# Last feed-forward of a two-layer streaming encoder: two of seven sums per group added by VectorE, and state products over all 128 rows

## The chip, the cores and the metric

The kernel runs on one core of a Trainium2 chip. The metric is device time in microseconds of one execution; lower is better. One further execution was recorded by the hardware profiler, and all rows below come from that one.

The engines are named as in the profile: PE is TensorE (PEld its weight loads), DVE is VectorE, ACT is ScalarE, POOL is GpSimd, and SP is SyncE, which here only issues DMAs.

## What is computed

Two layers of an encoder are applied to 640 token rows (512 of a new stream, 8 x 16 of running streams) of width 1024. Each layer is a feed-forward, a mixer and another feed-forward, and every sub-layer is wrapped in a layer norm. The change lies in the last feed-forward, and in the sample states of the second layer's mixer, which are computed beside it:

```python
def swiglu(x, w_gate, w_up, w_down):
    return (jax.nn.silu(x @ w_gate) * (x @ w_up)) @ w_down
...
x = layer_norm(ALPHA * x + 0.5 * swiglu(x, ffn_w_gate[l, 1], ffn_w_up[l, 1], ffn_w_down[l, 1]),
               ln_g[l, 2], ln_b[l, 2])
...
h_new = h * jnp.exp(cs[:, -1])[..., None, None] + jnp.einsum('bsgr,bsgn,bsgrp->bgrpn', to_end, b_c, x_c)
```

The inner width of the feed-forward, 2816, is 22 tiles of 128. In `h_new`, each of 4 head groups and 8 running streams has a state of 128 x 512 and 16 new tokens.

## The kernel before

All matrices are fp32. Each is split into a high and a low part, and a product is three matmuls: high x high, low x high, high x low. ACT casts the high part (line 94) and DVE subtracts for the low part (line 95). The activations stay in SBUF: `xt` with channels on partitions, and `yacc`, the running sum with tokens on partitions, five token tiles of 128 by 1024.

A feed-forward (`ffn`) goes over the 22 inner tiles: the first two by themselves, then five groups of four. Gate and up projections are made for two tiles at a time with Strassen's scheme in seven products instead of eight (`matrix`, line 356). The down projection of a group of four is made while the next group's weights arrive. In three of the four feed-forwards (`SEVEN`), the groups but the last use seven products too: `down7`. The last feed-forward, `ffn3`, has four such groups.

`down7` first makes token tile 4 in the plain way (line 506, summed on line 509). The other four token tiles are two pairs: `tp` 0 holds tiles 0 and 1, `tp` 1 holds tiles 2 and 3. The seven products `p` come in the order 1, 2, 5, 6, 3, 7, 4, each for `tp` 0 and then `tp` 1, six matmuls of 128x512 each (line 488). They share three accumulators per pair: `x` (products 1, 6, 7, 4), `w` (5, 3) and `z` (2). `x` and `w` come from the four PSUM banks of kind `b`, `z` from those of kind `a`. After each product, `add` puts the accumulator as it stands onto one half `j` of one token tile of `yacc`; only then may the next product of the chain go on accumulating in it. The tiles and halves for the products in their order are, for `tp` 0: (0, 0), (0, 0), (1, 1), (0, 1), (0, 1), (1, 1), (1, 0).

`add` has two ways:

- for `tp` 1 (`t // 2` is 1): one DVE instruction reads PSUM, scales and adds to `yacc` (line 496);
- for `tp` 0: ACT copies the scaled accumulator to a buffer `ev` (line 499), and POOL sends a DMA that adds it to `yacc` (line 500). Where side work runs (`few`, in the first and the last feed-forward) there are two `ev` buffers, elsewhere three. A DMA that adds to a tile's half waits for an earlier one on the same half to land.

Beside `ffn3` runs `ssd_states`, a generator that is moved on one step at a `tick` (in `down7` after product 5 and after product 3, and before it). It goes over 4 head groups x 2 x 2, 16 steps; a step loads rows for two streams, `h` 0 and 1, into `xb`: at rows 64h, three blocks of 16 rows (high x high, high x low, low x high: x parts in columns 0 to 511, b parts in 512 to 639). For each of the two streams it then makes one fp32r product over 48 rows, rows 64h to 64h + 47 of `xb` (line 1149), into a bank of kind `b`; ACT scales the old state `h0` in eight pieces (line 1152), DVE adds (line 1153), and SP stores it (line 1154).

The order of instructions on each engine is fixed when the kernel is built, by a scheduler that goes by estimated durations; each engine then runs its list in order.

Of the kernel before, what the change touches and what calls it, by code (L numbers as in the profile page):

```python
# [9 lines left out]
F32 = mybir.dt.float32  # L10
F32R = mybir.dt.float32r
# [24 lines left out]
def kernel(ctx: ExitStack, tc: tile.TileContext, I, O, phases=PHASES):  # L36
    nc = tc.nc

    def pool(name, bufs=1, stack=ctx, **kw):
        return stack.enter_context(tc.tile_pool(name=name, bufs=bufs, **kw))  # L40
# [24 lines left out]
    def bank_a():  # L65
        return bank("a")

    def bank_b():
        return bank("b")
# [27 lines left out]
    def raw_tile():  # L97
        return pools["raw"].tile([128, 1024], F32, name="raw")
# [4 lines left out]
    def two_units():  # L103
        return pools["w"].tile([128, 2, 2, 512], F32R, name="w")

    def split2(w, src):

        return split(w[:, :, 0], w[:, :, 1], src.rearrange("p (j c) -> p j c", j=2))
# [19 lines left out]
    def mm3(ps, lhs, rhs):  # L128
        n = 3 * len(lhs)
        k = 0  # L130
        for (wh, wl), (xh, xl) in zip(lhs, rhs):
            for a, b in ((wh, xh), (wl, xh), (wh, xl)):
                state["pe"] = nc.tensor.matmul(ps, a, b, start=(k == 0), stop=(k == n - 1)).ins  # L133
                k += 1
# [76 lines left out]
    def ffn(i, ph, last, side=None):  # L211
# [4 lines left out]
        with ExitStack() as st:  # L216
            wk = pool(f"ffn{i}_wk", 1, st, reuse_waits="tile")
            few = side is not None
            steps = side(wk) if side is not None else iter(())

            def tick(where):

                if ph == "ffn0" and where in range(NT):
                    for _ in range(2 if (fs[0], where) == (14, 4) else 1):
                        with tc.issue_after(state["acc"]):
                            next(steps, None)
                elif ph == "ffn3" and where in ("gate", "up", 0, 2, 4):
                    with tc.issue_after(state["silu"]):
                        next(steps, None)
# [48 lines left out]
            for r in range(2):  # L278
                w = load_w(I["w_gate"][i, 2 + r])
                first[r] = g_row()  # L280
                for c in range(2):
                    p = bank_a()[:, :Q]
# [166 lines left out]
            def down7(fs):  # L449


                raws, direct = {}, {}
                for f in fs:
                    raws[f] = raw_tile()
                    nc.sync.dma_start(raws[f], I["w_down"][i, f])
                for f in fs:
                    direct[f] = two_units()
                    split2(direct[f], raws[f])

                for f in fs[::2]:  # L460
                    (b11, b12), (b21, b22) = ((r[:, :512], r[:, 512:]) for r in (raws[f], raws[f + 1]))
                    V.tensor_tensor(b22, b22, b12, op=ALU.subtract)
                    V.tensor_tensor(b12, b12, b11, op=ALU.subtract)
                    V.tensor_tensor(b11, b22, b11, op=ALU.add)
                    V.tensor_tensor(b21, b21, b11, op=ALU.subtract)
                T = {}
                for r in range(2):
                    for f in fs[::2]:
                        T[f + r] = two_units()
                        split2(T[f + r], raws[f + r])  # L470

                def left(f, p, tp):
                    tok = lambda k, a: ht[f + k][:, :, 256 * tp + 128 * a:256 * tp + 128 * a + 128]
                    if p in (1, 2, 4):
                        return tok(*{1: (0, 0), 2: (1, 0), 4: (1, 1)}[p])
                    o = 256 * {5: 0, 6: 1, 7: 2, 3: 3}[p] + 128 * tp
                    return hs[f][:, :, o:o + 128]

                def right(f, p):
                    return {1: direct[f][:, 0], 2: direct[f + 1][:, 0], 3: direct[f + 1][:, 1],  # L480
                            6: T[f][:, 0], 5: T[f][:, 1], 4: T[f + 1][:, 0], 7: T[f + 1][:, 1]}[p]

                def product(ps, tp, p, first):
                    n = 0
                    for f in fs[::2]:
                        a, b = left(f, p, tp), right(f, p)
                        for u, v in ((0, 0), (1, 0), (0, 1)):
                            nc.tensor.matmul(ps, a[:, u], b[:, v], start=(first and n == 0), stop=(n == 5),  # L488
                                             skip_group_check=True)
                            n += 1  # L490

                def add(ps, t, j):

                    if t // 2:
                        ya = yacc[:, t, j * 512:j * 512 + 512]
                        V.scalar_tensor_tensor(ya, ps, 0.5 / ALPHA, ya, op0=ALU.mult, op1=ALU.add)  # L496
                        return
                    e = wk.tile([128, 512], F32, name="ev", bufs=2 if few else 3)
                    nc.scalar.mul(e, ps, 0.5 / ALPHA)  # L499
                    nc.gpsimd.dma_start(yacc[:, t, 512 * j:512 * j + 512], e, accum_op=ALU.add)  # L500

                t = NT - 1
                tick(0)
                for j in range(2):
                    pb = bank_a()
                    mm3(pb, [(ht[f][:, 0, t * 128:t * 128 + 128], ht[f][:, 1, t * 128:t * 128 + 128]) for f in fs],
                        [(direct[f][:, j, 0], direct[f][:, j, 1]) for f in fs])
                    ya = yacc[:, t, j * 512:j * 512 + 512]
                    state["acc"] = V.scalar_tensor_tensor(ya, pb, 0.5 / ALPHA, ya, op0=ALU.mult, op1=ALU.add).ins
                x, w = ([bank_b() for _ in range(2)] for _ in range(2))  # L510
                z = [bank_a() for _ in range(2)]
                for p, ps, a, j in ((1, x, 0, 0), (2, z, 0, 0), (5, w, 1, 1), (6, x, 0, 1), (3, w, 0, 1), (7, x, 1, 1),
                                    (4, x, 1, 0)):
                    for tp in range(2):
                        product(ps[tp], tp, p, p in (1, 2, 5))
                        add(ps[tp], 2 * tp + a, j)
                    if p in (5, 3):
                        tick(2 if p == 5 else 4)

# [605 lines left out]
    def ssd_states(wk):  # L1125

        el8 = wk.tile([128, 4, 8, 8], F32, name="el8")
        nc.sync.dma_start(el8.rearrange("p g b h -> p g (b h)"), ssd["el"])
        for g, b2, q in ((g, b2, q) for g in range(4) for b2 in range(2) for q in range(2)):

            xb = wk.tile([128, 640], F32, name="xb", bufs=1)
            for h in range(2):
                for r, (sx, sb) in enumerate(((0, 0), (0, 1), (1, 0))):
                    rows = slice(64 * h + 16 * r, 64 * h + 16 * r + 16)
                    t0 = 64 * h + 32 * b2 + 16 * q
                    src = lambda s, a, b: ssd["xb"][g][s, t0:t0 + 16, a:b]
                    if sx == sb:
                        nc.sync.dma_start(xb[rows], src(sx, 0, 640))
                    else:
                        nc.sync.dma_start(xb[rows, 0:512], src(sx, 0, 512))  # L1140
                        nc.sync.dma_start(xb[rows, 512:640], src(sb, 512, 640))
            for h in range(2):
                n = 4 * h + 2 * b2 + q
                h0 = wk.tile([128, 512], F32, name="h0", bufs=1)
                nc.sync.dma_start(h0, I["ssd_h0"][g, n])
                yield
                rows = slice(64 * h, 64 * h + 48)
                pst = bank_b()
                nc.tensor.matmul(pst, xb[rows, 512:640].bitcast(F32R), xb[rows, 0:512].bitcast(F32R),  # L1149
                                 start=True, stop=True)  # L1150
                for k in range(8):
                    nc.scalar.mul(h0[:, 64 * k:64 * k + 64], h0[:, 64 * k:64 * k + 64], el8[:, g, n, k:k + 1])  # L1152
                nc.vector.tensor_tensor(h0, h0, pst, op=ALU.add)
                nc.sync.dma_start(O["ssd_s"][g, n], h0)
# [391 lines left out]
    for ph in phases:  # L1546
        last = ph == phases[-1]
        if ph.startswith("ffn"):
            ffn(int(ph[3]), ph, last, sides.get(ph))
        elif ph == "mix0":  # L1550
            mixer0(ph, last)
        else:
            mixer1(ph, last)
            if "ffn3" not in phases:
                with ExitStack() as st:
                    for _ in ssd_states(pool("ssd", 1, st, reuse_waits="tile")):
                        pass
# [112 lines left out]
```

## Time and profile before

| | |
|---|---|
| Time, median of 3 runs | 2623.69 us (2619.67 to 2629.86) |
| Profiled execution, time | 2620.05 us |
| Profiled execution, span of the trace | 2618.4 us |
| Last feed-forward in the trace | from about 2150 us to the end |
| Its four `down7` groups | near 2262 to 2292, 2346 to 2376, 2430 to 2460, 2517 to 2547 us |
| State products, line 1149 | 32, from 2191.9 to 2557.1 us |
| ACT copies of line 499, whole kernel | 84, median 0.597 us |
| Adding DMAs of line 500, whole kernel | 84, from issue to landing 3.2 / 4.2 / 8.0 us (least, median, most) |

A row of the timeline gives the start in us from the start of the span, the duration, the engine, the line of the kernel, the operation and "output <- input"; in square brackets, how long the engine stood idle before it and what ended that. A matmul's row gives the rows and columns of its weights (128\*128) and then the moving operand. Matmuls overlap, so the distance from start to start counts for them, not the duration. The granted clock is TensorE's, 1.00 at full speed.

### The profile page before, as it was taken

The page shows a single profiled execution, that of the slowest core. Times are in us where ns is not written, and L with a number is a line of the kernel's source. Part 1 is how long each engine was busy: PE and PEld are TensorE (multiplying, and loading weights), DVE is VectorE, ACT ScalarE, POOL GpSimd, SP SyncE. Part 2 cuts the span into 40 slices and gives each one's busy share as a digit, 9 for nine tenths or more (in the row PEclk, how much of TensorE's full clock was granted, in tenths as well). Part 3 has the DMA queues.
Part 4 walks back from the last instruction along what each step waited for, and adds up shares of the span by engine and source line. Part 5 has one row for each costly group of instructions (what it writes and reads, how often), then busy time and mean ns, then how long its engine had stood idle before and what let it go on. Part 6 is the DMA issues. An engine that isn't in the chain of part 4 may idle for free. (4 is left out here: it accounts for less than half of the span.)

```text
span 2618.4 us, 41048 instructions
## 1 busy us (share of the span) xinstructions
PE 2532.5 (97%) x15529; PEld 2291.1 (88%) x15529; DVE 2071.7 (79%) x3770; ACT 1312.2 (50%) x2632; POOL 310.0 (12%) x440
## 2 busy tenths in 40 slices
PE   9999999999969999999999999999999999999998
PEld 8999999887658999998999999889999879898887
DVE  7788877667858888887888887777686898787778
ACT  4444344345523555553455554566564544666562
POOL 0000003010021000003000002211111240000001
PEclk9999999999979999999999999999999999999999
DMA  5332334542211334443144433456464722545552
GB/s 180 105 105 91 104 110 138 183 146 75 81 61 49 97 93 125 111 127 108 50 109 124 110 103 121 126 182 220 123 205 140 241 67 89 155 149 149 152 161 97
DMA packets 177846, 324.80 MB, mean 124 GB/s; under 512 B 20416, under 2 KB 91200, under 8 KB 177136
## 3 DMA queue, kind: packets, MB, share of 16 engines
q1 hardware_dynamic: 163792, 293.83, 35.0%
q0 software_dynamic: 13856, 28.35, 5.6%
q8 instruction: 122, 2.00, 0.3%
q14 instruction: 76, 0.62, 0.1%
HBM read 259.56 MB, written 40.54 MB: 115 GB/s over the span
## 5 line engine op out<-in xcount | busy, mean ns | idle before, releaser
L95 DVE TENSOR_TENSOR w<-raw,w 128x512 fp32r<-128x512 f32 (+1 forms) x617 | 553.5, 920 | 95.0 <-ACT w L94 94.1
L94 ACT CAST w<-raw 128x512 fp32r<-128x512 f32 (+1 forms) x617 | 466.0, 794 | 221.1 <-DVE raw L335 75.4
L133 PE MATMUL bank<-xhi,w 128*128 128x256 f32 (+2 forms) x2528 | 555.9, 312 | 14.3 <-ACT xhi L94 7.2
L356 PE MATMUL bank<-xhi,w 128*128 128x320 f32 x2432 | 544.1, 310 | 2.5 <-ACT mx L367 2.2
L133 PEld LDWEIGHTS bank<-xhi,w 128*128 128x128 f32 x2528 | 421.8, 189 | 26.2 <-ACT xhi L94 8.1
L356 PE MATMUL bank<-T,w 128*128 128x320 f32 x2736 | 427.0, 309 | 0.7 <-DVE s L393 0.5
L356 PEld LDWEIGHTS bank<-xhi,w 128*128 128x128 f32 x2432 | 406.4, 188 | 11.9 <-ACT mx L367 5.1
L356 PEld LDWEIGHTS bank<-T,w 128*128 128x128 f32 x2736 | 406.3, 188 | 3.3 <-ACT mx L367 1.2
L133 PE MATMUL bank<-xlo,w 128*128 128x256 f32 (+2 forms) x1264 | 391.3, 310 | 3.7 <-DVE xlo L95 3.6
L356 PE MATMUL bank<-xlo,w 128*128 128x320 f32 x1216 | 375.0, 308 | 0.0
L133 PE MATMUL bank<-w,h 128*128 128x512 f32 x1488 | 348.6, 391 | 0.0
L133 PEld LDWEIGHTS bank<-w,h 128*128 128x128 f32 x1488 | 276.5, 188 | 58.8 <-issue 1.2
L133 PEld LDWEIGHTS bank<-xlo,w 128*128 128x128 f32 x1264 | 238.6, 189 | 6.1 <-DVE xlo L95 4.7
L356 PEld LDWEIGHTS bank<-xlo,w 128*128 128x128 f32 x1216 | 228.1, 188 | 0.4
L500 POOL DMA_DIRECT2D yacc<-ev x84 | 73.0, 897 | 1019.9 <-ACT ev L499 828.6
L367 ACT COPY mx<-bank 128x320 f32<-128x320 f32 x228 | 96.0, 423 | 113.5 <-PE bank L356 111.8
L488 PE MATMUL bank<-w,hs 128*128 128x512 f32 x576 | 142.8, 408 | 0.0
L488 PEld LDWEIGHTS bank<-w,hs 128*128 128x128 f32 x576 | 113.6, 198 | 26.4 <-issue 2.1
L95 DVE TENSOR_TENSOR w<-sw,w 128x1024 fp32r<-128x1024 f32 x76 | 92.9, 1223 | 50.0 <-ACT w L94 49.7
L94 ACT CAST w<-sw 128x1024 fp32r<-128x1024 f32 x76 | 79.8, 1049 | 72.3 <-DVE sw L335 71.2
L496 DVE SCALAR_TENSOR_TENSOR yacc<-bank,yacc 128x512 f32<-128x512 f32 x84 | 57.3, 687 | 67.0 <-PE bank L488 67.0
L208 DVE SCALAR_TENSOR_TENSOR yacc<-bank,yacc 128x512 f32<-128x512 f32 x120 | 81.9, 686 | 35.1 <-PE bank L133 34.6
(416 smaller groups left out, 3531.8 us busy)
## 6 DMA issues: line engine op xcount, KB each, us to landing
raw<-in_w_gate_dram SPq DMA_DIRECT2D x88, 512.0 KB, 4.0
raw<-in_w_up_dram SPq DMA_DIRECT2D x88, 512.0 KB, 4.1
raw<-in_w_down_dram SPq DMA_DIRECT2D x88, 512.0 KB, 3.7
raw<-in_m_in_dram SPq DMA_DIRECT2D x52, 512.0 KB, 4.6
yacc<-ev POOLq DMA_DIRECT2D x84, 256.0 KB, 4.2
raw<-in_m_out_dram SPq DMA_DIRECT2D x24, 512.0 KB, 3.8
csb<-cs_d SPq DMA_DIRECT2D x20, 512.0 KB, 5.3
h<-in_ssd_h_dram SPq DMA_DIRECT2D x16, 512.0 KB, 5.7
```

The costliest lines, as they stand in the source:

```text
L94: nc.scalar.copy(hi, src)
L95: return nc.vector.tensor_tensor(lo, src, hi.bitcast(F32), op=ALU.subtract)
L133: state["pe"] = nc.tensor.matmul(ps, a, b, start=(k == 0), stop=(k == n - 1)).ins
L208: state["acc"] = nc.vector.scalar_tensor_tensor(ya, pb, scale, ya, op0=ALU.mult, op1=ALU.add).ins
L356: nc.tensor.matmul(ps, A[p][:, a, k * 128:k * 128 + 128], B[p][b][:, k, :], start=(first and n == 0), stop=(n == 11), skip_group_check=True)
L367: nc.scalar.copy(e[n], ps)
L488: nc.tensor.matmul(ps, a[:, u], b[:, v], start=(first and n == 0), stop=(n == 5), skip_group_check=True)
L496: V.scalar_tensor_tensor(ya, ps, 0.5 / ALPHA, ya, op0=ALU.mult, op1=ALU.add)
L500: nc.gpsimd.dma_start(yacc[:, t, 512 * j:512 * j + 512], e, accum_op=ALU.add)
```

## The change

Two edits, both only in the last feed-forward.

First, in `add`, products 6 and 7 of the first pair of token tiles take the DVE way too where `few` is set. Of the feed-forwards with side work only `ffn3` uses `down7`, so this is 2 sums in each of 4 groups: 8 copies on ACT and 8 adding DMAs become 8 DVE instructions of line 496.

Second, the state products read all 128 rows. The x parts go to `xrow`, 128 x 512, the b parts to `brow`, one 128 x 128 block for each `h`. Both are set to zero once by DVE. Only rows 64h to 64h + 47 of block `h` of `brow` are ever loaded, so the others stay zero and the product over 128 rows gives the same sum. Each 16-row block is now two loads, so a step has twelve loads where it had ten.

```diff
-                def add(ps, t, j):
+                def add(ps, t, j, p):
-                    if t // 2:
+                    if t // 2 or few and p in (6, 7):
                         ya = yacc[:, t, j * 512:j * 512 + 512]
                         V.scalar_tensor_tensor(ya, ps, 0.5 / ALPHA, ya, op0=ALU.mult, op1=ALU.add)
                         return
...
                         product(ps[tp], tp, p, p in (1, 2, 5))
-                        add(ps[tp], 2 * tp + a, j)
+                        add(ps[tp], 2 * tp + a, j, p)
...
+        xrow = wk.tile([128, 512], F32R, name="xrow", bufs=1)
+        brow = wk.tile([128, 2, 128], F32R, name="brow", bufs=1)
+        nc.vector.memset(xrow.bitcast(F32), 0.0)
+        nc.vector.memset(brow.bitcast(F32), 0.0)
         for g, b2, q in ((g, b2, q) for g in range(4) for b2 in range(2) for q in range(2)):
-            xb = wk.tile([128, 640], F32, name="xb", bufs=1)
             for h in range(2):
                 for r, (sx, sb) in enumerate(((0, 0), (0, 1), (1, 0))):
...
-                    if sx == sb:
-                        nc.sync.dma_start(xb[rows], src(sx, 0, 640))
-                    else:
-                        nc.sync.dma_start(xb[rows, 0:512], src(sx, 0, 512))
-                        nc.sync.dma_start(xb[rows, 512:640], src(sb, 512, 640))
+                    nc.sync.dma_start(xrow[rows].bitcast(F32), src(sx, 0, 512))
+                    nc.sync.dma_start(brow[rows, h].bitcast(F32), src(sb, 512, 640))
...
-                rows = slice(64 * h, 64 * h + 48)
                 pst = bank_b()
-                nc.tensor.matmul(pst, xb[rows, 512:640].bitcast(F32R), xb[rows, 0:512].bitcast(F32R),
-                                 start=True, stop=True)
+                nc.tensor.matmul(pst, brow[:, h], xrow, start=True, stop=True)
```

The scheduler orders the last feed-forward anew. Three places of the first `down7` group show how; groups 1 and 3 are ordered alike, and so are 2 and 4.

ACT, before, from the copy of product 1 (line 499) to the cast of the weight sum `sw` for the next projection; the lines 1152 are the eight scalings of one state, the lines 94 are weight casts:

```order
L499 ACTIVATE ev<-bank 128x512
L1152 ACTIVATE h_22667<-h_22667,el_21897 128x64 x3
L94 CAST w<-raw 128x2x512 x3
L1152 ACTIVATE h_22667<-h_22667,el_21897 128x64 x5
L499 ACTIVATE ev<-bank 128x512 x2
L94 CAST w_22937<-raw 128x512
L94 CAST w<-raw 128x2x512
L499 ACTIVATE ev<-bank 128x512 x2
L94 CAST w<-sw 128x2x512
```

The same stretch of ACT with the change (the scaling is on line 1151 there):

```order
L499 ACTIVATE ev<-bank 128x512
L94 CAST w<-raw 128x2x512 x3
L1151 ACTIVATE h_22675<-h_22675,el_21897 128x64 x8
L499 ACTIVATE ev<-bank 128x512 x2
L94 CAST w_22943<-raw 128x512
L94 CAST w<-raw 128x2x512
L499 ACTIVATE ev<-bank 128x512
L94 CAST w<-sw 128x2x512
```

The copy of product 6 is gone, so that of product 3 stands alone ahead of the cast of `sw`; and all eight scalings stand between the casts and the copies of products 2 and 5, where three of them stood ahead of the casts.

PE, before, from product 5 of the group on; `w,hs` are the matmuls of products 5, 6, 3 and 7, line 1149 the state products, line 356 the next projection:

```order
L488 MATMUL bank<-w,hs 128x512 x34
L1149 MATMUL bank<-xb 128x512
L488 MATMUL bank<-w,hs 128x512 x9
L1149 MATMUL bank<-xb 128x512
L488 MATMUL bank<-w,hs 128x512 x5
L356 MATMUL bank<-xhi,w 128x320 x2
```

The same stretch of PE with the change; `w,h` are the matmuls of product 4:

```order
L488 MATMUL bank<-w,hs 128x512 x34
L1149 MATMUL bank<-xrow,brow 128x512
L488 MATMUL bank<-w,hs 128x512 x8
L1149 MATMUL bank<-xrow,brow 128x512
L488 MATMUL bank<-w,hs 128x512 x6
L488 MATMUL bank<-w,h 128x512 x12
L356 MATMUL bank<-xhi,w 128x320 x2
```

The first state product keeps its place behind 34 of the 48 matmuls. Product 4 now follows product 7 at once; before, nine matmuls of the next projection stood between them.

DVE, before, from the addition of the preceding state to the second sum of product 7 (line 496 is the adding instruction, line 335 the weight sums, line 95 the low parts):

```order
L1153 TENSOR_TENSOR h_22667<-h_22667,bank 128x512
L496 SCALAR_TENSOR_TENSOR yacc<-bank,yacc 128x512 x2
L95 TENSOR_TENSOR w_22937<-raw,w_22937 128x512
L496 SCALAR_TENSOR_TENSOR yacc<-bank,yacc 128x512
L95 TENSOR_TENSOR w<-raw,w 128x2x512
L335 TENSOR_TENSOR sw<-raw 128x512
L335 TENSOR_TENSOR sw<-sw,raw 128x512
L496 SCALAR_TENSOR_TENSOR yacc<-bank,yacc 128x512
L95 TENSOR_TENSOR w<-sw,w 128x2x512
L335 TENSOR_TENSOR raw<-raw,sw 128x512
L496 SCALAR_TENSOR_TENSOR yacc<-bank,yacc 128x512
```

The same stretch of DVE with the change:

```order
L1152 TENSOR_TENSOR h_22675<-h_22675,bank 128x512
L496 SCALAR_TENSOR_TENSOR yacc<-bank,yacc 128x512 x2
L95 TENSOR_TENSOR w_22943<-raw,w_22943 128x512
L496 SCALAR_TENSOR_TENSOR yacc<-bank,yacc 128x512
L95 TENSOR_TENSOR w<-raw,w 128x2x512
L335 TENSOR_TENSOR sw<-raw 128x512
L335 TENSOR_TENSOR sw<-sw,raw 128x512
L496 SCALAR_TENSOR_TENSOR yacc<-bank,yacc 128x512 x2
L95 TENSOR_TENSOR w<-sw,w 128x2x512
L496 SCALAR_TENSOR_TENSOR yacc<-bank,yacc 128x512
```

The two sums behind the state addition are now those of product 5 (`tp` 1) and product 6 (`tp` 0); behind line 335 stand product 3's (`tp` 1) and product 7's (`tp` 0) together, and product 7's second sum follows the low part of `sw`.

## The prediction

> **What bounds the kernel now.** I read the page's first part, then the last feed-forward alone: busy time by windows, who waits for whom on PE, the timeline round one wait. Line 1 gives TensorE's share of the span; the others are stretches of the last feed-forward (length, then busy us of PE, PEld, DVE, ACT, POOL, granted clock, DMA share, GB/s).
>
> ```profile
> PE 2532.5 (97%) x15529; PEld 2291.1 (88%) x15529; DVE 2071.7 (79%) x3770; ACT 1312.2 (50%) x2632; POOL 310.0 (12%) x440
> 2262.00:2292.00 30.00, 25.73 (x110) 20.59 (x109) 21.20 (x29) 15.82 (x33) 6.09 (x7) 0.94 0.70 179
> 2292.00:2346.00 54.00, 54.00 (x344) 50.90 (x343) 46.98 (x73) 36.11 (x83) 0.00 (x0) 1.00 0.44 139
> 2346.00:2376.00 30.00, 27.32 (x111) 21.72 (x110) 20.60 (x27) 16.14 (x34) 6.07 (x7) 0.89 0.79 197
> 2430.00:2460.00 30.00, 25.62 (x103) 19.91 (x103) 20.04 (x28) 15.26 (x32) 5.19 (x6) 0.89 0.66 175
> 2517.00:2547.00 30.00, 26.69 (x109) 21.21 (x108) 20.57 (x27) 16.22 (x34) 6.06 (x7) 0.89 0.78 199
> ```
>
> TensorE is the bound: between the seven-product groups (2292 to 2346) it has no idle time. The four 30-us windows hold one group each, and there it idles 4.27 + 2.68 + 4.38 + 3.31 = 14.64 us, at a mean clock below 1. The longest of PE's waits from 2160 to 2584 (total us, times, longest) says for whom:
>
> ```profile
> PE bank L1149 <- ACT ev L499: 14.6, 4, 4.4
> ```
>
> All of it is one wait per group: the state product of line 1149 needs a `b` bank, and the bank that comes free is the one that ACT reads for product 3. Round the fourth wait (start, us, engine, line, tile; behind it the idle time and its releaser):
>
> ```profile
> 2523.73 7.87 PE L488 MATMUL bank<-w,hs 128*128 128x512 f32 x34
> 2534.91 0.79 PE L1149 MATMUL bank<-xb 48*128 48x512 f32 x1 [3.31 <-ACT ev L499]
> ...
> 2528.08 0.59 ACT L499 ACTIVATE ev<-bank 128x512 f32<-128x512 f32 x1
> 2532.79 0.60 ACT L499 ACTIVATE ev<-bank 128x512 f32<-128x512 f32 x1 [4.12 <-DMA yacc<-ev]
> 2534.26 0.60 ACT L499 ACTIVATE ev<-bank 128x512 f32<-128x512 f32 x1
> ...
> 2520.80 0.87 POOL L500 DMA_DIRECT2D yacc<-ev  x1 [59.16 <-ACT ev L499]
> 2528.29 1.76 POOL L500 DMA_DIRECT2D yacc<-ev  x2 [6.61 <-ACT w L94]
> ```
>
> The three ACT rows are the copies of products 5, 6 and 3 for the first tile pair; the POOL rows send product 1's addition, then those of products 2 and 5. There are two `ev` buffers: product 6 (2532.79) waits until the addition of product 2, sent at 2528.29, has landed, and product 3 (2534.26) stands behind it on ACT. The product of line 1149 starts 0.05 us after that copy ends.
>
> **Part 1: sums 6 and 7 on DVE.** Without product 6 on ACT, product 3 is the fourth user of `ev` and takes the buffer that product 6 took, at its time. So the bank is free when the copy of product 6 ended. The same pairs of copies in groups 1 to 3, with two earlier rows of group 1:
>
> ```profile
> 2266.65 0.83 ACT L1152 ACTIVATE h<-h,el 128x64 f32<-128x64 f32 x3 [1.24 <-DVE raw L464]
> 2271.43 1.05 ACT L499 ACTIVATE ev<-bank 128x512 f32<-128x512 f32 x2
> 2278.55 0.60 ACT L499 ACTIVATE ev<-bank 128x512 f32<-128x512 f32 x1 [3.64 <-DMA yacc<-ev]
> 2280.18 0.60 ACT L499 ACTIVATE ev<-bank 128x512 f32<-128x512 f32 x1 [1.03 <-DMA yacc<-ev]
> ...
> 2361.18 0.60 ACT L499 ACTIVATE ev<-bank 128x512 f32<-128x512 f32 x1 [3.62 <-DMA yacc<-ev]
> 2362.85 0.60 ACT L499 ACTIVATE ev<-bank 128x512 f32<-128x512 f32 x1
> ...
> 2447.88 0.60 ACT L499 ACTIVATE ev<-bank 128x512 f32<-128x512 f32 x1 [3.88 <-DMA yacc<-ev]
> 2449.38 0.60 ACT L499 ACTIVATE ev<-bank 128x512 f32<-128x512 f32 x1 [0.90 <-DMA yacc<-ev]
> ```
>
> Earlier by 1.63, 1.67, 1.50 and 1.47 us. In groups 1 and 3 the order of ACT takes half back: the three scalings that used a gap (2266.65, 0.83 us) now stand with the other five behind the casts, so the copies of products 2 and 5 (2271.43), the addition and its landing come some 0.83 us later. I take 0.8 + 1.67 + 0.67 + 1.47 = **4.6 us** of idle time gone (6.3 without that loss; all 14.6 if the landing also came sooner). The waits left are estimated at 3.5, 1.0, 3.7 and 1.8 us. What is late next is the landing of product 2's addition, which waits for product 1's on the same rows of `yacc`; no part of the change touches that pair.
>
> DVE gets 8 additions (four groups, two sums, one tile of the pair):
>
> ```profile
> L496 DVE SCALAR_TENSOR_TENSOR yacc<-bank,yacc 128x512 f32<-128x512 f32 x28 | 18.8, 686 | 22.6 <-PE bank L488 22.6
> ```
>
> That is 8 x 0.686 = 5.5 us, in windows in which DVE is busy 20 to 21 of 30 us. Product 7's addition waits for product 5's to have landed (same tile and half): group 1 has that at 2280.18, when product 3's copy got product 5's buffer, and product 7 would end about 2281.3, so it passes with about 1 us to spare. Behind it on DVE stand the lower half of the cast sum `sw` and product 7's second sum, for which product 4 waits; between the two lie six matmuls, 1.4 us. I take 0; if that cover goes, 0.7 us a group, 2.7 in all. The two memsets are once, below 1 us.
>
> **Part 2: the clock.** After each wait TensorE runs at half clock (first four rows: the slow stretch in each group). The last three: a short gap elsewhere, a somewhat longer one, and what followed that.
>
> ```profile
> 2281.25:2284.65 3.40, 3.40 (x9) 2.71 (x9) 2.13 (x3) 2.38 (x9) 0.85 (x1) 0.50 0.36 61
> 2363.50:2369.95 6.45, 6.45 (x15) 4.76 (x16) 4.18 (x6) 3.48 (x10) 1.72 (x2) 0.50 0.69 149
> 2450.05:2455.15 5.10, 5.10 (x11) 3.33 (x11) 2.42 (x3) 3.31 (x10) 0.86 (x1) 0.50 0.49 85
> 2534.90:2540.45 5.55, 5.54 (x12) 4.08 (x13) 4.38 (x6) 3.66 (x10) 0.85 (x1) 0.50 0.63 140
> ...
> 1802.00:1804.00 2.00, 0.27 (x3) 0.04 (x2) 1.97 (x7) 1.18 (x4) 0.79 (x4) 1.00 0.60 143
> ...
> 2134.00:2136.50 2.50, 0.43 (x3) 0.32 (x3) 2.50 (x3) 0.00 (x0) 2.42 (x3) 1.00 0.00 0
> 2137.25:2140.65 3.40, 3.22 (x9) 2.52 (x9) 2.87 (x8) 0.00 (x0) 0.48 (x1) 0.59 0.00 0
> ```
>
> 20.5 us at 0.50 cost half of it, 10.25 us. A gap of 1.73 us (2.00 - 0.27) left the clock at 1; one of 2.07 did not. So the edge lies between. Group 2 (1.0 us left) keeps its clock, saving 6.45/2 = 3.2. Group 4 (1.8) lies nearer to 1.73 than to 2.07: 5.55/2 = 2.8 saved. Groups 1 and 3 (3.5, 3.7) stay slow: 0. I take **6.0 us**; ends: 0 and 10.25.
>
> **Part 3: 128 rows.** A 48-row product in an unbroken run, and the pitch of full ones:
>
> ```profile
> 2326.09 1.92 PE L356 MATMUL bank<-T,w 128*128 128x320 f32 x12
> 2327.95 0.50 PE L1149 MATMUL bank<-xb 48*128 48x512 f32 x1
> 2328.38 0.56 PE L356 MATMUL bank<-xhi,w 128*128 128x320 f32 x2
> ...
> 2518.29 5.60 PE L488 MATMUL bank<-w,h 128*128 128x512 f32 x24
> L1149 PEldq EVENT_SEMAPHORE  x75: 51/51/51, 2188.2 to 2554.5; - x75
> ```
>
> Twelve 320-column matmuls start every (1.92 - 0.31)/11 = 0.146 us, the last at 2327.70; two pitches on, with a full 512-column matmul between, the next would start 0.146 + (5.60 - 0.39)/23 = 0.37 later; it starts 0.68 later. So a 48-row product costs 0.30 us more than its columns. There are 32: 28 at 0.29 and 4 behind a wait, where only the gap after it counts (0.2): **8.9 us**. Ends: 0, if the gap came from the semaphore waits, which remain, and 8.9; the 75 waits of 51 ns explain at most 75/32 x 0.051 = 0.12 of the 0.30, so I take the upper end.
>
> The Trainium skill has a rule each way. "TensorEngine Tiling (Array Packing)", section Tiling Modes, says that changing the tiling mode drains TensorE: by that all 8.9 us go, and the gap on both sides in these rows agrees. "TensorE: Matmul & The Clock Gate", section Why this matters for your kernels, says that a single matmul with 32 rows takes the time of one with 128: by that alone padding saves 0, and the total is 10.6 instead of 19.5.
>
> The loads for it: twelve per step in place of ten, at the queue's pace here, and what a product waited for them before:
>
> ```profile
> L1141 SPq DMA_DIRECT2D xb<-xb_d x64: 303/420/1426, 2154.4 to 2541.6; - x64
>   DMA xb<-xb_d: 0.4, 1
> DMA to landing us min/median/max: 1.6/1.9/4.9
> ```
>
> 32 more loads are 32 x 0.42 = 13.4 us of SP's queue over 400 us. Three of the `brow` loads now wait only for the first product of the step before, so nine instead of ten follow its second. In PE's order the first product of 11 of the 16 steps stands 10 to 47 matmuls later. I take 0; end: 0.8 us (two issues) for each of 16 steps, 13.
>
> **Sum.** 4.6 + 6.0 + 8.9 = 19.5 us off the profiled execution's 2620.05: 2600.6. The median of the runs shown is 3.6 us above that execution; part of such scatter should recur, so I say **2602 us**.
>
> **Rivals.**
> - *The gap is not the rows' doing* (waits on semaphores, or a short product costs this anyway): only parts 1 and 2, 10.6 us off, 2609.5. For it: more waits stand ahead of first products. Against: the gap behind the product has no wait. 0.15.
> - *The clock drops in groups 2 and 4 all the same* (the edge is not one of length alone): 13.5 off, 2606.5. The four waits and the gap of 2.07 us lost the clock, that of 1.73 did not, and 1.8 is close to both. 0.13.
> - *The waits vanish* (the additions land sooner with fewer of them, and the clock stays): up to 33.8 off, 2586. Against: products 1 and 2 still add to the same rows one after the other. 0.08.
> - *Slower: PE waits for `xrow` and `brow`.* Each step's first product waits for twelve loads; if it comes 1.2 us late in each of the 16 steps the gain is gone, and from 2.0 us on the kernel is 0.5% slower, about 2637. One wait of 0.4 us before says that these loads land close to their use; SP's two extra issues give 0.84, the rest would need landings far above the median of 1.9. 0.04.
> - *It does nothing* (another engine takes PE's place at once, most likely DVE, 79% busy): within 5 us of before. 0.05.
>
> The forecast itself, 2596 to 2608, has 0.55. The range is 2590 to 2612: it leaves out the vanished waits, the last two rivals and a little more, 2 in 10. A measurement of this kernel tells about 0.5%, 13 us, from no change; that is 2610.6 against the median. Faster: 0.78, same 0.18, slower 0.04.
>
> **What would show it.** PE's wait on line 1149 for `ev` falls from 14.6 to about 10 us, and the clock of group windows 2 and 4 reads 1.00. The product of line 1149 reads 128 rows, with a pitch of 0.23. SP shows no wait of PE on `xrow` or `brow`. I am wrong if PE waits for DVE at products 7 or 4, if the slow stretches remain in all four groups, or if the gap of 0.3 us round line 1149 remains.

## The result, and the profile after

| | before | changed | ratio (95% interval) |
|---|---|---|---|
| Time, median | 2622.78 us (5 runs, 2619.67 to 2629.86) | 2605.43 us (5 runs, 2602.44 to 2612.86) | 0.9939 (0.9916 to 0.9961) |
| Profiled execution | 2620.05 us | 2605.15 us | |

The change gains 17.4 us, 0.6%, where 2602 us was forecast. In the profiled executions it is 14.9 us, so the working, which came to 19.5 us against that same execution, was 4.6 us too high.

The changed kernel's engines over the whole span, and below them the four 30-us windows that hold one seven-product group each, with the columns of the prediction (length, busy us of PE, PEld, DVE, ACT, POOL, granted clock, DMA share, GB/s):

```profile
PE 2516.9 (97%) x15529; PEld 2288.3 (88%) x15529; DVE 2075.9 (80%) x3780; ACT 1309.2 (50%) x2624; POOL 308.5 (12%) x432
```

```profile
2264.50:2294.50 30.00, 26.56 (x121) 22.21 (x121) 23.89 (x33) 14.67 (x30) 4.37 (x5) 0.94 0.70 170
2344.50:2374.50 30.00, 28.05 (x129) 23.52 (x128) 24.36 (x34) 17.78 (x39) 4.30 (x5) 0.94 0.71 193
2423.50:2453.50 30.00, 26.78 (x118) 21.93 (x117) 23.27 (x31) 15.79 (x34) 4.37 (x5) 0.94 0.67 178
2506.00:2536.00 30.00, 27.26 (x132) 22.63 (x131) 24.67 (x34) 17.95 (x41) 4.29 (x5) 1.00 0.77 210
```

POOL has 8 additions fewer to send and DVE ten instructions more (eight sums, two memsets). TensorE idles 3.44, 1.95, 3.22 and 2.74 us in the four windows, 11.35 in place of 14.64, and only the fourth keeps its clock. TensorE's waits in the last feed-forward of the changed kernel (total us, times, longest):

```profile
PE bank L1149 <- ACT ev L499: 9.6, 4, 3.4
PE bank L133 <- ACT xhi L94: 7.7, 1, 7.7
PE bank L488 <- DVE yacc L496: 1.4, 1, 1.4
```

The wait that the change was aimed at is 5.0 us shorter (14.6 before). The second row is new at this size: at the start of the last feed-forward TensorE waits 7.7 us for ACT's cast of `xhi`, the high part of the layer's input. Its place in the timeline of the changed kernel (start, us, engine, line, tile; in brackets the idle time before it and its releaser):

```profile
2151.89 1.03 PE L195 MATMUL bank<-ident,yacc 128*128 128x128 f32 x8
2152.88 0.33 SPq L323 DMA_DIRECT2D raw<-in_w_up_dram  x1
...
2154.73 0.38 ACT L272 ACTIVATE hf<-bank 128x256 f32<-128x256 f32 x1
2155.97 0.48 DVE L1133 MEMSET xrow<- 128x512 f32 x1
2156.46 0.27 DVE L1134 MEMSET brow<- 128x256 f32 x1
2156.49 0.33 SPq L1141 DMA_DIRECT2D xrow<-xb_d  x1
...
2159.21 0.62 ACT L94 CAST w<-raw 128x512 fp32r<-128x512 f32 x1 [4.10 <-DMA raw<-in_w_up_dram]
...
2160.04 1.06 ACT L94 CAST xhi<-bank 128x512 fp32r<-128x512 f32 x2
2160.67 1.97 PE L133 MATMUL bank<-xhi,w 128*128 128x384 f32 x5 [7.75 <-ACT xhi L94]
```

And the same place in the kernel before:

```profile
2155.22 1.04 PE L195 MATMUL bank<-ident,yacc 128*128 128x128 f32 x8
...
2157.06 0.58 ACT L94 CAST xhi<-bank 128x512 fp32r<-128x512 f32 x1
...
2157.69 1.14 PE L133 MATMUL bank<-xhi,w 128*128 128x384 f32 x5 [1.43 <-ACT xhi L94]
...
2159.68 0.37 SPq L323 DMA_DIRECT2D raw<-in_w_up_dram  x1
```

The last transposes (line 195) end and TensorE needs their cast `xhi`. Before, ACT makes the first of these casts 0.80 us after them, and TensorE idles 1.43 us. With the change ACT has a weight cast of `w_up` ahead of it in its list; it stands 4.10 us for the weights to land, and the two `xhi` casts that TensorE needs stand behind it, though their input is there from 2152.92. On SP's queue the load of `w_up` has moved from behind the state rows' loads to ahead of them: those loads now need the memsets, which DVE makes only at 2155.97.

The stage from those transposes to the end takes 451.6 us (2603.5 - 2151.89) in place of 463.2 (2618.4 - 2155.22); the other 3.3 us of the 14.9 lie before it, in work that the change leaves as it was. That part is luck: TensorE worked 25.1 us at half clock there in place of 30.8, which at half of it is 2.8 us. The 11.6 us by terms:

| | us |
|---|---|
| wait of line 1149 for `ev`, 14.6 to 9.6 | -5.0 |
| half clock in the four groups: half of the 20.93 us worked at it before, and of 10.24 now | -5.3 |
| 48 rows to 128, as estimated (0.29 and 0.2 each; the 0.29 measured below) | -8.9 |
| new: product 4 waits for DVE's sum of product 7 (1.4), and a line 488 for `h` (0.3) | +1.7 |
| new: wait for `xhi` at the start, 1.43 to 7.75 | +6.3 |
| new: half clock right behind that wait, half of the 3.2 us worked at it | +1.6 |
| sum | -9.6 |

2.0 us of the 11.6 are in none of these terms. Another profiled execution of the same changed kernel (a0 below) has 453.1 us in this stage, and a third (a1) 452.4: two executions differ by up to 1.5 us, and where the 2.0 come from stays open.

### The profile page after: what moved, and what is told of

Its sections match the earlier page's. It is cut to its first block, busy times and chain, and to the rows that moved or that the text cites. A ratio compares the mean times of both kernels' runs of the same rounds, so it can differ in the third digit from the quotient of the medians.

```text
span 2603.5 us, 41070 instructions
## 1 busy us (share of the span) xinstructions
PE 2516.9 (97%) x15529; PEld 2288.3 (88%) x15529; DVE 2075.9 (80%) x3780; ACT 1309.2 (50%) x2624; POOL 308.5 (12%) x432
## 5 line engine op out<-in xcount | busy, mean ns | idle before, releaser
L500 POOL DMA_DIRECT2D yacc<-ev x76 | 66.1, 898 | 1014.7 <-ACT ev L499 944.4
L496 DVE SCALAR_TENSOR_TENSOR yacc<-bank,yacc 128x512 f32<-128x512 f32 x92 | 62.7, 688 | 59.4 <-PE bank L488 59.2
L208 DVE SCALAR_TENSOR_TENSOR yacc<-bank,yacc 128x512 f32<-128x512 f32 x120 | 81.9, 686 | 34.5 <-PE bank L133 34.0
```

The costliest lines, as they stand in the source:

```text
L208: state["acc"] = nc.vector.scalar_tensor_tensor(ya, pb, scale, ya, op0=ALU.mult, op1=ALU.add).ins
```

## The experiments

All these kernels compute the whole output. Each ratio is against the kernel before on the same chip; e1 to e4 shared one chip, a0 and e5 to e7 a second, e8, a1 and e9 a third.

**The parts by themselves: e1, the sums alone.** The kernel before with only the first edit:

```diff
-                    if t // 2:
+                    if t // 2 or few and p in (6, 7):
```

> The sums of products 6 and 7 on DVE alone, the state products over 48 rows as before. My theory (the sums shorten the bank wait of line 1149, and with it the half-clock stretches; the rows edit alone lengthened the wait for xhi at the start of the last feed-forward): PE's wait of line 1149 for ev 9 to 11 us in place of 14.6, half-clock stretches in at most three of the four groups, the wait for xhi at the start of the last feed-forward 1.4 us as before, 0.30 us of gap round each 48-row product as before; 7 to 11 us faster than before. Rival (the rows edit brought all of the gain, the sums only moved work): within 3 us of before.

Measured: 2612.74 us (2610.15 to 2616.41) against 2620.86; ratio 0.9964 (0.9951 to 0.9978), 9.4 us. Its waits of TensorE in the last feed-forward:

```profile
PE bank L1149 <- ACT ev L499: 8.9, 4, 3.1
PE bank L133 <- ACT xhi L94: 2.0, 1, 2.0
```

5.7 us of wait for `ev` gone, and no long wait at the start (2.0 us, where 1.4 was expected). The clock still drops in all four groups, against the expectation, but for 16.0 busy us in place of 20.9: 2.4 us. Together 8.1 of the 9.4. So the sums bring a gain by themselves, and the start's wait is not theirs.

**e2, the rows alone** (the changed kernel with the first edit undone):

```diff
-                    if t // 2 or few and p in (6, 7):
+                    if t // 2:
```

> State products over 128 rows alone, the sums on ACT and DMA as before. My theory: the 0.3 us of gap round each product goes (about 9 us off), and the wait for xhi at the start of the last feed-forward grows from 1.4 to about 7.7 us with some half clock behind it (6 to 8 us on); the wait of line 1149 for ev stays at 14 to 15 us; net 0 to 4 us faster than before. Rival (the long wait at the start comes from the sums edit or from chance): wait 1.4 us at the start and 8 to 10 us faster.

Measured: 2619.2 us (12 runs, 2614.64 to 2622.98); ratio 0.9988 (0.9979 to 0.9996), 3.1 us. TensorE's wait at the start there:

```profile
PE bank L133 <- ACT xhi L94: 6.5, 1, 6.5
```

The start's wait comes with the rows, and with it a stretch of 6.8 us at half clock. That is 5.1 us more wait than before, and half of what TensorE worked in the slow stretch is lost, 2.5 us: 7.6 us given back of the 8.9 gained. The 1.3 us that are left are within 2 us of the 3.1 measured.

**e3, the gap round the product.** The changed kernel with its product cut to 48 rows again:

```diff
-                nc.tensor.matmul(pst, brow[:, h], xrow, start=True, stop=True)
+                rows = slice(64 * h, 64 * h + 48)
+                nc.tensor.matmul(pst, brow[rows, h], xrow[rows], start=True, stop=True)
```

> The changed kernel, but its products read rows 64h to 64h+47 of the same tiles, so loads, zeros and semaphore waits are as in the changed kernel. Drain theory: from the start of a product of line 1149 to the next matmul 0.43 to 0.44 us again in place of 0.23, and a late start of about 0.1; some 9 us slower than the changed kernel, near 2614. Semaphore rival (the gap was due to the waits on five loads): no gap behind the products, as in the changed kernel, and its time.

One product in an unbroken run, first of e3, then of the changed kernel:

```profile
2304.80 1.92 PE L356 MATMUL bank<-T,w 128*128 128x320 f32 x12
2306.65 0.50 PE L1150 MATMUL bank<-xrow,brow 48*128 48x512 f32 x1
2307.08 0.56 PE L356 MATMUL bank<-xhi,w 128*128 128x320 f32 x2
```

```profile
2325.95 1.92 PE L356 MATMUL bank<-T,w 128*128 128x320 f32 x12
2327.71 0.39 PE L1149 MATMUL bank<-xrow,brow 128*128 128x512 f32 x1
2327.94 0.45 PE L356 MATMUL bank<-xhi,w 128*128 128x320 f32 x2
```

From the first of the twelve to the matmul behind the product: 2.28 us with 48 rows, as before (2328.38 - 2326.09 = 2.29), and 1.99 with 128. The product starts 0.09 us sooner (1.85 to 1.76 after the twelve begin) and the next follows it 0.23 us later in place of 0.43. So the number of rows makes the gap, on both sides. Over all 32 products the median distance to the next matmul, at full clock, is 0.43 us in the kernel before, e1 and e3, and 0.23 in every kernel with 128 rows. That waits on semaphores make it fell: TensorE's queue has 75 of them at this line in the kernel before, which has the gap, and 73 in the changed kernel, which has not. The time of e3, 2610.1 us in one run where 2614 was expected, says less: its ACT list in groups 1 and 3 came out in another order, and the wait for `ev` was 4.8 us instead of 9.6.

**e4, e8, e9: the memsets.** The changed kernel, and e2, with the memsets on POOL instead of DVE:

```diff
-        nc.vector.memset(xrow.bitcast(F32), 0.0)
-        nc.vector.memset(brow.bitcast(F32), 0.0)
+        nc.gpsimd.memset(xrow.bitcast(F32), 0.0)
+        nc.gpsimd.memset(brow.bitcast(F32), 0.0)
```

> The changed kernel with the two memsets on POOL, so that xrow and brow are loaded ahead of the first w_up weights again, and ACT's first w_up cast stands behind the casts of xhi. My theory (ACT stood waiting for w_up's load with the casts of xhi behind it): the wait of PE for xhi at the start of the last feed-forward falls from 7.7 to about 1.4 us; 5 to 8 us faster than the changed kernel, 22 to 26 us faster than before. Rival (DVE's memsets or the load itself held PE up, whatever ACT's order): the wait stays above 5 us, time as the changed kernel.

Measured: 2605.14 us (2597.8 to 2605.84), ratio 0.9934 (0.9921 to 0.9948). The wait for `xhi` fell to 2.7 us, but the time is 15.7 us below the kernel before where 22 to 26 were expected, the changed kernel was not run beside it on this chip, and the intervals of the two ratios overlap: inconclusive as a time. Hence the same kernel again as e9, beside the changed kernel as a1, and e2 with the memsets on POOL as e8:

> The changed kernel, beside the next one on the same chip: 0.993 to 0.996 of before.

> The changed kernel with the memsets on POOL once more, now beside the changed kernel. My theory: the wait at the start shrinks by some 5 us in every execution, while the half-clock stretches come and go with where a wait lies on a grid of 3.41 us, so medians differ by 3 to 8 us. Rival: the medians agree within 2 us.

> State products over 128 rows alone, with the memsets on POOL, the sums on ACT and DMA as before. My theory (the rows edit saves 9 us and gave 5 to 8 of them back through ACT's wait for w_up's load): 7 to 11 us faster than before, against 3.1 with the memsets on DVE; PE's wait for xhi at the start 1.4 to 2.7 us. Rival (the gap of 0.3 us was time that PE would have idled elsewhere): within 4 us of before.

| | median us | ratio (95%) | wait for `xhi`, us |
|---|---|---|---|
| a1, changed | 2608.52 (2604.75 to 2611.57) | 0.9949 (0.9936 to 0.9961) | 6.3 |
| e9, memsets on POOL | 2601.53 (2598.15 to 2603.21) | 0.9921 (0.9909 to 0.9934) | 1.4 |
| e8, rows alone, memsets on POOL | 2612.41 (2604.59 to 2620.1) | 0.9965 (0.9954 to 0.9977) | 1.4 |

The start of the last feed-forward in the timeline of e9:

```profile
2152.08 0.43 SPq L1141 DMA_DIRECT2D xrow<-xb_d  x1
...
2153.87 1.04 PE L195 MATMUL bank<-ident,yacc 128*128 128x128 f32 x8
...
2155.71 0.58 ACT L94 CAST xhi<-bank 128x512 fp32r<-128x512 f32 x1
...
2158.80 0.37 SPq L323 DMA_DIRECT2D raw<-in_w_up_dram  x1
```

POOL clears the tiles early, so the rows' loads go first and `w_up` again behind them (2158.80), and ACT's list is as before the change: `xhi` follows the transposes at once. In the lists as built, without times, ACT at this place in the changed kernel and then in e9:

```
L272 ACTIVATE hf<-bank 128x256
L94 CAST w_22091<-raw 128x512
L94 CAST h<-hf 128x256
L94 CAST xhi<-bank 128x4x128 x2

L272 ACTIVATE hf<-bank 128x256
L94 CAST xhi<-bank 128x4x128
L94 CAST h<-hf 128x256
L94 CAST xhi<-bank 128x4x128
```

e9 is 7.0 us faster than a1, and its slowest run (2603.21) is faster than the fastest of a1 (2604.75). The rows alone go from 3.1 us of gain to 9.2 by the same move, each against the kernel before on its chip. So by the medians the memsets' place costs some 6 to 7 us.

**a0, e5, e6, e7: how many sums on DVE.** The changed kernel again (a0); product 1 on DVE too (e5); that with the memsets on POOL (e6); and all sums of the last feed-forward on DVE with the memsets on POOL (e7):

```diff
-                    if t // 2 or few and p in (6, 7):
+                    if t // 2 or few and p in (1, 6, 7):    # e5, e6
+                    if t // 2 or few:                       # e7
```

> The changed kernel itself, as the measure for the three beside it on the same chip. Every theory: 0.992 to 0.996 of before. PE's wait of line 1149 for ev 9 to 11 us, its wait for xhi at the start of the last feed-forward 6 to 8 us; which groups run at half clock behind their wait may differ from the first record.

> The changed kernel with product 1's sum of the first pair on DVE too (sums 1, 6, 7). My theory (what is late in each group is the landing of product 2's addition, which waits for product 1's on the same half): product 2 and 5 then take the two ev buffers at once and their additions go out without a wait; PE's wait of line 1149 for ev falls from about 9.6 to at most 4 us and at most one group runs at half clock; 5 to 10 us faster than the changed kernel. Rival (the additions are slow because of the other loads in flight, not because of each other): the wait stays at 8 us or more and so does the time.

> Sums 1, 6, 7 on DVE and the memsets on POOL. My theory: the two gains add, 9 to 15 us faster than the changed kernel, wait for xhi at the start 1.4 to 2.7 us. Rival (a chip state, not the wait at the start, sets that part): as the same kernel with the memsets on DVE, within 2 us.

> All seven sums of the first pair on DVE in the last feed-forward, memsets on POOL: no ev copy and no adding DMA is left there, DVE has 20 additions more than the changed kernel (13.7 us). My theory (DVE has room: 21 of 30 us busy in the group windows): no wait on ev, waits of PE for DVE's sums below 6 us in all, time within 4 us of the kernel with sums 1, 6, 7. Rival (DVE becomes the bound of the groups): PE waits more than 10 us for DVE and the kernel is slower than the changed one.

| | median us | ratio (95%) |
|---|---|---|
| a0, changed | 2609.05 (2605.82 to 2613.11) | 0.9945 (0.9931 to 0.9959) |
| e5, sums 1, 6, 7 | 2608.75 (2604.82 to 2609.73) | 0.9944 (0.9931 to 0.9957) |
| e6, the same, memsets on POOL | 2602.32 (2598.63 to 2604.61) | 0.992 (0.9906 to 0.9934) |
| e7, all sums, memsets on POOL | 2597.84 (2596.36 to 2600.12) | 0.9906 (0.9892 to 0.992) |

TensorE's waits in e5, and then in e7:

```profile
PE bank L133 <- ACT xhi L94: 7.8, 1, 7.8
PE bank L1149 <- ACT ev L499: 5.6, 4, 2.3
PE bank L488 <- DVE yacc L496: 3.3, 3, 2.1
```

```profile
PE bank L488 <- DVE yacc L496: 3.9, 4, 1.6
PE bank L133 <- ACT xhi L94: 2.7, 1, 2.7
```

e5 missed its expectation. The wait for `ev` was halved (10.7 in a0, 5.6 here; at most 4 was expected), and two groups ran at half clock instead of at most one. In groups 2 and 4 the wait fell from 4.1 us to 1.3, in groups 1 and 3 from 6.6 to 4.3. But the median is that of a0, 0.3 us apart. 2.7 of the 5.1 us went to the waits for DVE (1.4 longer than in a0) and for `xhi` (1.3). The rest can't be placed: a0's profiled execution was the slowest of its six. e6 is 6.4 us faster than e5, again the memsets; it missed its expectation too, 6.7 us below a0 instead of 9 to 15, since e5 had gained nothing that shows. In e7 no sum goes by a DMA, so there is no wait for `ev`; what is late next is DVE, 3.9 us in four waits. Two of its group windows:

```profile
2257.00:2287.00 30.00, 29.73 (x141) 24.75 (x141) 28.14 (x40) 14.76 (x36) 0.00 (x0) 1.00 0.42 129
2335.00:2365.00 30.00, 27.72 (x126) 22.38 (x125) 26.72 (x39) 14.18 (x34) 0.00 (x0) 1.00 0.44 143
```

DVE is busy 28.14 and 26.72 of 30 us, and TensorE keeps its full clock. That DVE becomes the bound there and the time goes back up fell: e7 is the fastest of all, 11.2 us below the changed kernel on the same chip, 25.6 below the kernel before, and 4.5 below e6, a little more than the 4 expected at most.

## Why the prediction was right, and where it was not

**The waits (4.6 us).** The size was right, what is late next only in part. The copy of product 3 took product 6's place. In the changed kernel, groups 1 to 4, with two POOL rows that send the addition of product 2 (the first also that of product 5):

```profile
2274.23 1.75 POOL L500 DMA_DIRECT2D yacc<-ev  x2 [5.51 <-ACT ev L499]
2281.31 0.60 ACT L499 ACTIVATE ev<-bank 128x512 f32<-128x512 f32 x1 [4.65 <-DMA yacc<-ev]
2281.96 0.50 PE L1149 MATMUL bank<-xrow,brow 128*128 128x512 f32 x1 [3.44 <-ACT ev L499]
...
2355.42 0.87 POOL L500 DMA_DIRECT2D yacc<-ev  x1 [5.81 <-DMA yacc<-ev]
2361.50 0.51 PE L1149 MATMUL bank<-xrow,brow 128*128 128x512 f32 x1 [1.95 <-ACT ev L499]
...
2442.40 0.50 PE L1149 MATMUL bank<-xrow,brow 128*128 128x512 f32 x1 [3.22 <-ACT ev L499]
...
2521.63 0.50 PE L1149 MATMUL bank<-xrow,brow 128*128 128x512 f32 x1 [1.00 <-ACT ev L499]
```

3.44, 1.95, 3.22 and 1.00 stood where 3.5, 1.0, 3.7 and 1.8 were estimated, 9.6 in place of 10. What is late next is the landing of product 2's addition, as was said. But it stands behind product 1's only in groups 2 and 4: group 2's POOL row is released by that landing, and in group 4 it came at 2516.4, 3.4 us after product 2's copy began. In groups 1 and 3, which have 6.7 of the 9.6 us, product 1's addition had landed before product 2's copy began on ACT (in group 1 at 2272.1; the copy began at 2273.34, behind the eight scalings). The two additions sent from 2274.23 on then took 7.0 and 7.7 us to land, with the DMA engines busy to 0.98. So e5, which takes product 1's addition away, could not remove these waits: it leaves 4.3 us in groups 1 and 3, where product 2's addition still took 6.4 and 6.2 us. That the other transfers in flight make it so slow was not tested.

**DVE's additions (0; 2.7 if the cover goes).** The cover went in one group, for 1.4 us (1.7 with a wait for `h`). Group 4 of the changed kernel:

```profile
2523.51 2.03 ACT L1151 ACTIVATE h<-h,el 128x64 f32<-128x64 f32 x8 [1.93 <-DVE yacc L496]
...
2525.57 0.69 DVE L1152 TENSOR_TENSOR h<-h,bank 128x512 f32<-128x512 f32 x1 [2.15 <-ACT h L1151]
2526.17 0.69 DVE L496 SCALAR_TENSOR_TENSOR yacc<-bank,yacc 128x512 f32<-128x512 f32 x1
2526.91 1.67 PE L488 MATMUL bank<-w,h 128*128 128x512 f32 x6 [1.44 <-DVE yacc L496]
```

DVE was not short of time: it stood 2.15 us for ACT's scaling of a state, and product 7's sum, for which product 4 waits, stood behind that state's addition (line 1152). The working counted DVE's busy time ahead of product 4, not what DVE itself waits for there.

**The clock (6.0 us).** The size held, 5.3; the reason did not. Group 4 kept its clock as said (2.9 us). Group 2 lost it after a wait of 1.95 us, but for one stretch in place of two (1.5 saved), and so did group 3 (0.9), which was costed at no change. The edge is not one of length alone (last section), so this was the second rival's condition, half fulfilled. That the sum of the clock terms came out 0.7 us from the 6.0 is luck. The time, 2605.4 us, lies nearer to this rival's 2606.5 than to 2602, but not for the rival's reason: the missing time went mostly into the start's wait.

**128 rows (8.9 us).** Right, by e3's pitch and by e8: 9.2 us (6.0 to 12.1) for the rows alone once the start's wait is out. The first rival (the gap is not the rows' doing) fell. Of the two rules of the Trainium skill, that of "TensorEngine Tiling (Array Packing)", section Tiling Modes, that a change of mode drains TensorE, agrees with 0.43 against 0.23 us and with the later start. That of "TensorE: Matmul & The Clock Gate", section Why this matters for your kernels, does not hold for a lone product between full ones: by the same pitch 48 rows cost 0.29 us more than 128.

**The loads and the memsets (0 and below 1 us).** This is the step that failed. "I take 0" held for what it looked at: nowhere does TensorE wait for `xrow` or `brow`, the slower rival did not come. And the memsets do take 0.48 + 0.27 us. What they cost is their place: they hold the rows' loads on SP, the order around them turned, and ACT came to stand for `w_up` in front of the cast that TensorE needs. In this profile that is 6.3 us of wait and 1.6 of half clock; the medians of e9 and a1 put it at 7.0. It was to be seen beforehand in ACT's list at the start of the feed-forward, which the working did not look at because the memsets were costed by their duration.

**The sum.** Without that step the 19.5 us hold: by its ratio e9 gains 20.7 us (17 to 24), and e4 17. The traces agree for the stage from the transposes to the end, which leaves out the earlier work: 463.2 us before, 451.6, 453.1 and 452.4 in the three executions of the changed kernel, 443.2 and 442.6 in e4 and e9. That is 20.0 and 20.6 us less than before; each of these two executions was the fastest of its kernel's runs. The rivals "the waits vanish" and "it does nothing" fell. The changed kernel's three ratios, 0.9939, 0.9945 and 0.9949, are gains of 13 to 16 us: the forecast's sum less what the memsets' place costs, and close to the line of 0.5%. Luck had a part in how near the time came: 3.3 us of the profiled gain lie outside the stage, and the changed kernel's later medians, 2609.05 (a0) and 2608.52 (a1), lie just above the 2596 to 2608 of the forecast itself.

## What to carry to other kernels

Cost an instruction that runs once by what stands behind it on every queue, not by its duration: 0.75 us of memsets on a busy engine held the first loads of the rows, turned the order of two queues and cost some 7 us here; on an engine that was idle there they cost nothing that shows. When a change makes a scheduler order a stage anew, compare the lists at the stage's start too, where one instruction waiting for a DMA can stand in front of what the bound engine needs. And where a small matmul of few rows stands alone between full ones, filling its operands with zeros can be the cheaper product.

## What was not expected of the hardware

The granted clock changes on a fixed grid. In each of the 13 profiles (the kernel before, the changed one and the eleven runs) all changes between 1.00 and 0.50 fall on multiples of 3.413 us from a start that differs from execution to execution, to within 0.01 us. In the kernel before it drops at 2281.24, 2363.16 and 2448.49: 81.92 us is 24 of them, 85.33 is 25. Windows laid on that grid, in the kernel before, in the changed kernel, in e1 and in e4:

```profile
2277.82:2281.24 3.42, 0.41 (x1) 0.18 (x1) 0.00 (x0) 1.66 (x3) 0.85 (x1) 1.00 0.70 173
2281.24:2284.65 3.41, 3.41 (x9) 2.71 (x9) 2.13 (x3) 2.38 (x9) 0.85 (x1) 0.50 0.36 62
```

```profile
2276.53:2279.94 3.41, 1.98 (x9) 1.31 (x7) 2.87 (x4) 0.13 (x1) 0.00 (x0) 1.00 0.98 285
2279.94:2283.36 3.42, 1.40 (x6) 1.18 (x7) 0.40 (x1) 1.67 (x3) 0.84 (x1) 1.00 0.65 146
2283.36:2286.77 3.41, 3.41 (x10) 2.65 (x9) 2.02 (x3) 1.88 (x8) 0.00 (x0) 0.50 0.51 94
```

```profile
2359.64:2363.06 3.42, 1.93 (x8) 1.14 (x7) 3.14 (x5) 0.60 (x1) 0.61 (x1) 1.00 1.00 192
2363.06:2366.47 3.41, 3.41 (x10) 2.62 (x9) 1.59 (x3) 2.95 (x9) 0.25 (x1) 0.50 0.59 111
```

```profile
2435.00:2438.40 3.40, 1.54 (x7) 1.27 (x8) 1.24 (x3) 0.84 (x2) 0.88 (x1) 1.00 0.74 173
```

The changed kernel's 3.44 us gap is cut in two by the grid: the window with 1.43 us of it (3.41 - 1.98) is followed by full clock, the one with 2.02 by half. In e1 a window with 1.49 us idle was followed by half clock, in e4 one with 1.86 was not. Over all profiles, windows at full clock with 2.0 us idle or more were always followed by a drop, those below 1.3 never, and between the two both happened. The extremes are 1.32 us with a drop (e6, from 204.78, among short matmuls) and 1.95 without (the kernel before, from 799.85); what decides there stays open. A window already at half clock was followed by another after as little as 0.34 us idle (the kernel before, from 2363.16). So gaps of much the same length can cost nothing (2.65 us in group 1 of e6, cut by the grid into 1.65 and 1.00), one window at half speed (1.49 us in e1, for 1.7 us lost), or two (2.68 us in group 2 of the kernel before, for 3.2), by where they fall. The prediction's gap of 1.73 us was cut into 1.30 and 0.43, so that it kept the clock says nothing of an edge in length.

The start of the grid differs between executions of one kernel too (3.25, 0.19 and 2.95 us behind the start of the span in the changed kernel, a0 and a1), so this should be part of the spread between runs of one kernel. Ahead of the last feed-forward, where TensorE runs the same instructions in all 13 profiles, it worked between 21.1 and 34.2 us at half clock: by half of the difference, an estimate, up to 6.5 us between two executions.

The Trainium skill, "TensorE: Matmul & The Clock Gate", section What's actually happening, gives a free-running window of 3413 ns, and these runs agree. That one idle window is needed for the drop does not agree: in e1's first window above TensorE worked 1.93 of 3.42 us, and the clock dropped.
